# 38 of 43 k tiles of a down projection by seven products: four groups of eight and one of six, in place of a group of four and four of eight

## The chip, the cores and the metric

The kernel runs on one core of a Trainium2 chip. The metric is the device time of one execution in microseconds. Three runs of the kernel before gave 945.45, 945.89 and 946.0; the median is 945.89.

## The reference

One layer of a bidirectional encoder on 256 positions of width 2048, all in float32. Attention and a Fourier mix come first; the change lies in the feed-forward part, which takes some two thirds of the time:

```python
D_FF = ((8 * D_MODEL // 3 + 127) // 128) * 128      # 5504 = 43 x 128

def _conv_ffn(h, w_up, dw_w, dw_b, w_down):
    up = h @ w_up
    gate, val = up[..., :D_FF], up[..., D_FF:]
    gate = lax.conv_general_dilated(
        gate, dw_w, window_strides=(1,), padding=((CONV_WIDTH // 2, CONV_WIDTH // 2),),
        dimension_numbers=('NWC', 'WIO', 'NWC'), feature_group_count=D_FF) + dw_b
    act = jax.nn.gelu(gate, approximate=False) * val
    return act @ w_down
...
    x = x + _conv_ffn(_rmsnorm(x, norm2_g), w_up, dw_w, dw_b, w_down)
    return _rmsnorm(x, normf_g)
```

## The kernel before

**Precision.** Every float32 product is made from two parts of each operand: `hi`, the value rounded to the matmul's input type (a ScalarE copy, L180 or L961), and `lo`, the rest (a VectorE subtraction, L181 or L962). Three matmuls, hi by hi, hi by lo and lo by hi, give the result. Each weight is split so once, after its load, into one of three buffers for hi and one of three for lo.

**Items.** The feed-forward part is a list of items that `ff_items` (L84) writes out by the patterns of L72: `u` is an up unit, `s` a product of a group, `d` a late unit of the down projection. TensorE takes the items in that order.

- An up unit computes the gate or the value columns of one of the 43 k tiles (j): 16 matmuls of 512 columns with hi and 16 of 256 with lo (`still_weights`, L322; its argument `first` says how many of each kind go ahead of the strict alternation). Behind it `up_posts` (L1003) hangs the sums, the convolution, GELU and the product with the value.
- A group of 2n k tiles computes its part of the down projection as a two by two block product by seven products in place of eight, as Strassen's method does, once for each of two column pairs c. A product P1 to P7 or N3 to N5 is 3n matmuls of 512 columns (`by_parts`, L1066). Its stationary operands are sums of activation blocks (`operand`, `operand_sums`). Its weights are sums of four blocks a, b, c, d: these are loaded into a ring of two buffers by SP (`ring_load`, L940); the sum x is begun by VectorE (`first_sums`, L972) and goes on by DMAs that add to it, issued by POOL: d after the split of N5, c after the split of P6 (L965 to L968). P6 reads x after the first of these, N4 after the second. P1 and N5 gather in PSUM over all groups; the others are added up in SBUF after each (`product_out`), and `shared_out` (L1047) joins them at the end.
- The late k tiles go plainly, 24 matmuls a k tile over four column blocks (`moving_weights`, L310); `down_out` adds the result. The late units of c 0 and 1 gather on the banks of the products P2 and N4 of the last group.
- The last three k tiles (40 to 42) come after all items, by four column blocks and two row blocks: `last_product`, nine matmuls each, with final norm and output between them.

**Order.** After item n come, in this order, what was hung `beside` n, the split of item n + 2, and what was hung `behind` n (`ff_step`, L992). Loads of up, late and last weights go through three raw buffers; the load that takes a buffer is issued right behind the split that frees it (L182). The split of the fourth block of last weights (`split_last(3)`) is issued ahead of the third's, which comes with the step of item ("last", 0) after the first `last_product`.

Before, the groups are k tiles 0 to 3, 4 to 11, 12 to 19, 20 to 27 and 28 to 35; 36 to 39 are late.

Of the kernel before, what the change touches and what calls it, by code (L numbers as in the profile page):

```python
# [16 lines left out]
NK = D // P  # L17
# [43 lines left out]
OUT_ORDER += [(c, k) for c in (2, 3) for k in range(4)]  # L61


GROUPS = [(0, 2), (4, 4), (12, 4), (20, 4), (28, 4)]
LATE = list(range(36, 40))
LAST = list(range(40, NF))
PRODUCTS = [
    ["P1", "P7", "N5", "N3", "P6", "P2", "N4"], ["P1", "N5", "P7", "N3", "P6", "P2", "N4"]
]


PATTERNS = ["uuu" + "su" * 13 + "s"] * (len(GROUPS) - 1)  # L72
PATTERNS += ["uuu" + "su" * 6 + "sd" + "su" * 5 + "sdsdd"]


def group_of(j):

    for g, (first, n) in enumerate(GROUPS):
        if j < first + 2 * n:
            return (g, *divmod(j - first, n))  # L80
    return None


def ff_items():  # L84


    def ups(first, end):
        return [(kind, j) for j in range(first, end) for kind in ("gate", "val")]

    firsts = [first for first, _ in GROUPS] + [LATE[0], NF]  # L90
    items = ups(0, firsts[1])
    for g, pattern in enumerate(PATTERNS):
        todo = {
            "u": ups(firsts[g + 1], firsts[g + 2]),
            "s": [("product", g, c, p) for c in range(2) for p in PRODUCTS[c]],
            "d": [("down", c) for c in (0, 2, 1, 3)],
        }
        items += [todo[c].pop(0) for c in pattern]
        assert not (todo["u"] or todo["s"]), (g, todo)
    return items + [("last", c) for c in range(4)]  # L100
# [3 lines left out]
def block_kernel(  # L104
# [6 lines left out]
    w_in: bass.AP,  # L111
    w_out: bass.AP,
    w_up: bass.AP,
    w_down_two: bass.AP,
    w_down: bass.AP,
    w_down_late: bass.AP,
    w_down_last: bass.AP,
    normf_g: bass.AP,
# [16 lines left out]
    def bank(pool, name):  # L135
        return pool.tile([P, 512], F32, tag=pool.name, name=name)


    units = [(w_u_x[i], 2048) for i in range(4)] + [(w_in[i], 2048) for i in range(20)]
# [3 lines left out]
    items, up_index = ff_items(), {}  # L143
    for n, it in enumerate(items):
        if it[0] == "product":
            continue
        up_index[n] = len(units)
        if it[0] in ("gate", "val"):
            units.append((w_up[2 * it[1] + (it[0] == "val")], 2048))
            shifts.append((0, SHIFT))  # L150
            continue
        elif it[0] == "down":
            units.append((w_down_late[it[1]], 2048))
        else:
            units.append((w_down_last[it[1]], 512 * len(LAST)))
        shifts.append((0, 0))
    RAW = 3
    raws, halves = {}, {}
# [100 lines left out]
    ps = bank(dn, "ps_warm")  # L259
# [62 lines left out]
    def still_weights(hi, lo, ps, kk, first=(0, 0)):  # L322

        todo = [list(kk), list(kk)]
        order = [(i, todo[i].pop(0)) for i in range(2) for _ in range(first[i])]
        while todo[0] or todo[1]:
            order += [(i, todo[i].pop(0)) for i in range(2) if todo[i]]  # L330
        for n, (i, k) in enumerate(order):
            x = slice(0, S if i else 2 * S)
            nc.tensor.matmul(  # L333
                ps[:, x], (hi, lo)[i][:, k * P : (k + 1) * P], hk(k)[:, x],
                start=n == 0 and k == 0, stop=n == len(order) - 1 and k == NK - 1,
            )

    def hk(k):
        return hT[k // 4][:, k % 4, :]
# [18 lines left out]
    def at(when, i, f, *a):  # L358
        when.setdefault(i, []).append((f, a))
# [17 lines left out]
    for k in range(NK):  # L377
        c, q = k // 4, k % 4
        if q == 0:
            hi, lo = (t.rearrange("p (k c) -> p k c", k=4) for t in parts_of(c))  # L380
        n = 1 if c < 2 else 2
# [421 lines left out]
    for n, (c, kq) in enumerate(OUT_ORDER):  # L803
# [15 lines left out]
        if kq >= 2:  # L819
            part = "a" if kq == 2 else "f"  # L820
            ps = ps_a[c] if kq < 3 else ps_a[c, "f"]
# [47 lines left out]
    def val_mult(j):  # L869
        va, ge = sums_of.pop(f"v{j}"), gate_out.pop(j)  # L870
        if j >= LATE[0]:
            q = j - LATE[0]
            if q % 2 == 0:
                tag = ("va", "va", "op_P1", "op_N5")[q // 2]
                act["pair"] = fp.tile(
                    [P, 2, 512], F32R, tag=tag, name=f"act_{j}", bufs=3 if tag == "va" else 1
                )
            nc.vector.tensor_tensor(va, va, ge, ALU.mult)
            sums_of[j] = va
            act[j] = act["pair"][:, q % 2, :]  # L880
            return
        g, half, q = group_of(j)
        if q == 0:
            parts[g, half] = fp.tile([P, 4, S], F32, tag="va", name=f"va{g}k{half}", bufs=3)
        nc.vector.tensor_tensor(parts[g, half][:, q, :], va, ge, ALU.mult)
# [18 lines left out]
    def block_of(g, name):  # L904
        k, t = PLACE[name]
        return parts[g, k][:, 0 : GROUPS[g][1], t * P : (t + 1) * P]

    def operand(g, name):

        o = fp.tile([P, 2, 4, P], F32R, tag=f"op_{name}", name=f"op_{name}", bufs=1)  # L910
        o = o[:, :, 0 : GROUPS[g][1], :]
        a = block_of(g, name)
# [15 lines left out]

    ring, ring_tiles = [(g, c, w) for g in range(len(GROUPS)) for c in range(2) for w in "abdc"], {}
    ring_next = [0]  # L930

    def weights_of(g, c, w):
        n = c * 4 + "abcd".index(w)
        return w_down_two[n] if g == 0 else w_down[8 * (g - 1) + n]

    def ring_tile(g, tag, name, bufs):
        t = fp.tile([P, 2048], F32, tag=tag, name=name, bufs=bufs)
# [54 lines left out]
    def ff_step(n):  # L992
        todo, later[:] = list(later), []
        for f in todo:
            next(f, None)
        run(beside, n)
        split_item(n + 2)
        for f in todo:
            for _ in f:
                pass  # L1000
        run(behind, n)

    def up_posts(n, kind, j, ps):  # L1003
# [4 lines left out]
        else:  # L1008
            at(beside, n + 1, scaled_sum, ps, f"v{j}")
            at(beside, n + 2, val_mult, j)  # L1010
            if j + 1 in [first + 2 * n for first, n in GROUPS]:
# [9 lines left out]
                at(behind, n + 7, operand, g, "P6")  # L1021
            if j >= LATE[0]:
                at(behind, n + 2, act_parts, j)
# [109 lines left out]


    pair, joined = [], {}
    for q in range(2):
        kind, j = items[q]
        ps = bank(mm, f"ps_{kind}{j}")
        pair.append((ps, *halves.pop(n_front + q)))
        still_weights(*pair[q][1:], ps, range(12))  # L1140
        if q == 0:
            ff_step(0)
            turn_x(3)
            hT[:] = hT2
# [9 lines left out]
    for n, it in enumerate(items):  # L1154
        if n < 2:
            continue
        if it[0] == "last":
            break
        if n in (2, 3):
            ring_load()  # L1160
        if n == 5:
            pending.append(lambda: first_sums(0, 0))
        if it[0] in ("gate", "val"):
            kind, j = it
            ps = bank(mm, f"ps_{kind}{j}")
            still_weights(*halves.pop(up_index[n]), ps, range(NK))
            ff_step(n)
            up_posts(n, kind, j, ps)
            continue
        if it[0] == "product":  # L1170
            kind, g, c, p = it
            end = g == len(GROUPS) - 1
            if (c, p) in held:
                by_parts(held[c, p], parts[p], *halves.pop(it), GROUPS[g][1], g == 0, end)
            elif end and p in ("P2", "N4"):
                ps = joined[c, p] = bank(mm, f"ps_{p}{g}{c}")
                by_parts(ps, parts[p], *halves.pop(it), GROUPS[g][1], True, False)
            else:
                ps = bank(mm, f"ps_{p}{g}{c}")
                by_parts(ps, parts[p], *halves.pop(it), GROUPS[g][1], True, True)  # L1180
                at(beside, n + 1, product_out, g, c, p, ps)
            if end and p == ("N4", "P6")[c]:
                for q in range(3):
                    at(behind, n + 1 + (1 + c) * q, shared_out, c, q)
        else:
            kind, c = it
            hi, lo = halves.pop(up_index[n])
            if c < 2:
                ps = [joined.pop((c, p)) for p in ("P2", "N4")]
            else:  # L1190
                ps = [bank(mm, f"ps_l{c}{b}") for b in range(2)]
            for b in range(2):
                moving_weights(hi, lo, 512, LATE, act.get, b, ps[b], c >= 2, True)
            at(beside, n + 1, down_out, c, ps)
            if c == 1:
                gfb = fp.tile([P, D], F32, tag="sumw", name="gfb", bufs=1)
                nc.gpsimd.dma_start(gfb, normf_g.partition_broadcast(P))
        ff_step(n)
# [50 lines left out]
def _layout(inp):  # L1249
# [40 lines left out]
    def rows_by(tiles, cols):  # L1290
# [4 lines left out]
    downs = [  # L1295
        rows_by(range(k, k + m), c + n)
        for first, m in GROUPS
        for c in (0, 512)
        for k in (first, first + m)
        for n in (0, 1024)  # L1300
    ]
    late = [rows_by(LATE, 512 * c) for c in range(4)]
    dw = f(inp["dw_w"]).reshape(3, NF, P).transpose(2, 1, 0).reshape(P, 3 * NF)
# [21 lines left out]
        "w_in": win,  # L1325
        "w_out": wout,
        "w_up": wup,
        "w_down_two": np.stack(downs[:8]),
        "w_down": np.stack(downs[8:]),
        "w_down_late": np.stack(late),  # L1330
        "w_down_last": np.stack([rows_by(LAST, 512 * c) for c in range(4)]),
        "normf_g": f(inp["normf_g"]),
# [20 lines left out]
```

## Time and profile before

| what | us |
|---|---|
| median of three runs | 945.89 |
| the profiled execution | 945.47 |
| its span, first to last instruction | 943.7 |
| TensorE busy | 934.7 |
| VectorE busy | 759.8 |
| ScalarE busy | 541.4 |
| POOL busy | 50.6 |

The feed-forward part begins at 255.7 us of the span. In rows of instructions the first number is the start or, in groups, the line; the second is how long it took. In groups, the numbers behind the bar are busy time in us, the mean of one in ns, and the idle time before them with what ended it. In rows of stretches each engine has its busy time and its number of instructions; then come the granted TensorE clock, the busy share of the DMA engines and GB/s. Rows of DMA issues give the size of one and the median time in us from issue to landing. DVE is VectorE, ACT is ScalarE, PE is TensorE and PEld its weight loads.

### The profile page before, as it was taken

What the parts mean: (1) busy time and instruction counts of PE and PEld (TensorE: products, weight loads), DVE (VectorE), ACT (ScalarE), POOL (GpSimd) and SP (SyncE); (2) the same over time, 40 slices, a digit from 0 to 9 for tenths busy, and PEclk for the clock granted to TensorE, in tenths of its full rate; (3) what the DMA queues carried; (4) which work ended last, traced back from release to release, by engine and by line L of the source; (5) the groups of instructions that cost most, each with busy time, mean ns of one, the idle gap of its engine ahead of it and who ended that gap; (6) DMA issues with size and microseconds to landing.
All of it is one profiled execution on the core that took longest, in us unless ns stands there. A gap on an engine that the chain in (4) does not pass through costs nothing.

```text
span 943.7 us, 12802 instructions
## 1 busy us (share of the span) xinstructions
PE 934.7 (99%) x5069; PEld 809.9 (86%) x5069; DVE 759.8 (81%) x948; ACT 541.4 (57%) x659; POOL 50.6 (5%) x67
## 2 busy tenths in 40 slices
PE   9999999999999999999999999999999999999996
PEld 7889998888888888888888888888888888888885
DVE  7658877666677878799887997878989779989886
ACT  7756766454454564566555565555655556655542
POOL 0100000000000000000000000000000000000002
PEclk9999999999999999999999999999999999999999
DMA  9964444446456577877797778777787978779552
GB/s 365 308 224 150 163 147 166 142 171 223 179 220 207 187 238 239 273 249 250 234 276 256 244 228 288 236 262 230 258 246 240 302 234 267 226 244 290 178 178 90
DMA packets 33628, 214.86 MB, mean 228 GB/s; under 512 B 3712, under 2 KB 4224, under 8 KB 10016
## 3 DMA queue, kind: packets, MB, share of 16 engines
q1 hardware_dynamic: 29024, 184.55, 52.9%
q0 software_dynamic: 4544, 29.49, 16.4%
q8 instruction: 40, 0.66, 0.3%
q14 instruction: 20, 0.16, 0.0%
HBM read 211.93 MB, written 2.10 MB: 227 GB/s over the span
## 4 chain that ended last, share of the span: by engine, by line
PE 98%; DVE 1%; DMA 0%; issue 0%; ACT 0%; DVEq 0%; POOLq 0%; POOL 0%; ACTq 0%
PE ps_val L333 25%; PE ps_gate L333 25%; PE ps_q L333 7%; PE ps_P L1071 3%; PE ps_P L1072 3%; PE ps_P L1070 3%; PE ps_N L1071 3%; PE ps_N L1072 3%; PE ps_N L1070 3%; PE ps_a L318 2%; PE ps_a L316 2%; PE ps_k L333 2%; PE ps_a L317 2%; PE ps_s L637 1%; PE ps_o L709 1%; PE ps_ff L316 1%
## 5 line engine op out<-in xcount | busy, mean ns | idle before, releaser
L181 DVE TENSOR_TENSOR lo<-raw,hi 128x2048 fp32r<-128x2048 f32 (+1 forms) x129 | 293.4, 2275 | 40.5 <-ACT hi L180 40.3
L180 ACT ACTIVATE hi<-raw 128x2048 fp32r<-128x2048 f32 (+1 forms) x129 | 245.5, 1903 | 41.5 <-PE ps_a L317 13.5
L333 PE MATMUL ps_val<-hU,hi 128*128 128x512 f32 x688 | 236.6, 390 | 0.0
L333 PE MATMUL ps_gate<-hU,hi 128*128 128x512 f32 x688 | 236.5, 389 | 0.0
L333 PE MATMUL ps_val<-hU,lo 128*128 128x256 f32 x688 | 190.1, 276 | 0.0
L333 PE MATMUL ps_gate<-hU,lo 128*128 128x256 f32 x688 | 190.1, 276 | 0.0
L333 PEld LDWEIGHTS ps_val<-hU,hi 128*128 128x128 f32 x688 | 129.2, 188 | 27.0
L333 PEld LDWEIGHTS ps_gate<-hU,hi 128*128 128x128 f32 x688 | 129.2, 188 | 26.9
L333 PEld LDWEIGHTS ps_val<-hU,lo 128*128 128x128 f32 x688 | 129.2, 188 | 1.3
L333 PEld LDWEIGHTS ps_gate<-hU,lo 128*128 128x128 f32 x688 | 129.2, 188 | 1.3
L845 ACT ACTIVATE ft_g<-ps_gate 128x256 f32<-128x256 f32 x43 | 16.5, 384 | 123.8 <-PE ps_gate L333 123.8
L845 ACT ACTIVATE ft_v<-ps_val 128x256 f32<-128x256 f32 x43 | 16.5, 384 | 91.1 <-PE ps_val L333 91.1
L333 PE MATMUL ps_q<-hT,hi 128*128 128x512 f32 x192 | 65.2, 392 | 0.0
L1071 PE MATMUL ps_P<-hi_P,op_P 128*128 128x512 f32 x144 | 56.2, 390 | 0.0
L1070 PE MATMUL ps_P<-hi_P,op_P 128*128 128x512 f32 x144 | 56.1, 389 | 0.0
L1072 PE MATMUL ps_P<-lo_P,op_P 128*128 128x512 f32 x144 | 56.0, 389 | 0.0
L333 PE MATMUL ps_q<-hT,lo 128*128 128x256 f32 x192 | 51.1, 277 | 0.0
L962 DVE TENSOR_TENSOR lo_N<-sumw,hi_N 128x2048 fp32r<-128x2048 f32 (+1 forms) x20 | 41.5, 2076 | 9.4 <-ACT hi_N L961 9.2
L1071 PE MATMUL ps_N<-hi_N,op_N 128*128 128x512 f32 x108 | 42.1, 390 | 0.0
L1070 PE MATMUL ps_N<-hi_N,op_N 128*128 128x512 f32 x108 | 42.0, 389 | 0.0
L1072 PE MATMUL ps_N<-lo_N,op_N 128*128 128x512 f32 x108 | 42.0, 389 | 0.0
L333 PEld LDWEIGHTS ps_q<-hT,hi 128*128 128x128 f32 x192 | 35.2, 188 | 6.7
(380 smaller groups left out, 1584.2 us busy)
## 6 DMA issues: line engine op xcount, KB each, us to landing
raw<-in_w_up SPq DMA_DIRECT2D x86, 1024.0 KB, 5.7
raw<-in_w_in SPq DMA_DIRECT2D x20, 1024.0 KB, 4.9
raw<-in_w_out SPq DMA_DIRECT2D x16, 1024.0 KB, 4.8
sumw<-in_w_down POOLq DMA_DIRECT2D x16, 1024.0 KB, 8.3
raw<-in_w_down_late SPq DMA_DIRECT2D x4, 1024.0 KB, 6.2
raw<-in_w_down_last SPq DMA_DIRECT2D x4, 768.0 KB, 4.4
ux<-in_w_u_x SPq DMA_DIRECT2D x3, 768.0 KB, 9.4
xs<-in_x SPq DMA_DIRECT2D x4, 512.0 KB, 16.6
```

The lines of the kernel that those rows point to most:

```text
L180: nc.scalar.activation(hi[:, 0:n], raw[:, 0:n], AF.Copy)
L181: nc.vector.tensor_tensor(lo[:, 0:n], raw[:, 0:n], f32(hi[:, 0:n]), ALU.subtract)
L316: nc.tensor.matmul(ps, ah, wh, start=first and q == q0, stop=False)
L317: nc.tensor.matmul(ps, al, wh, start=False, stop=False)
L318: nc.tensor.matmul(ps, ah, wl, start=False, stop=last and q == q0 + len(kk) - 1)
L333: nc.tensor.matmul(ps[:, x], (hi, lo)[i][:, k * P : (k + 1) * P], hk(k)[:, x], start=n == 0 and k == 0, stop=n == len(order) - 1 and k == ...
L637: nc.tensor.matmul(ps[:, b * S : (b + 1) * S], qT[:, qo + b * P : qo + (b + 1) * P], kT[:, ko : ko + S], start=n == 0, stop=n == 2,)
L845: nc.scalar.activation(tmp, ps[:, S : 2 * S], AF.Copy)
L962: nc.vector.tensor_tensor(lo, src, f32(hi), ALU.subtract)
L1070: nc.tensor.matmul(ps, o[:, 0, p, :], hi[:, s], start=first and p == 0, stop=False)
L1071: nc.tensor.matmul(ps, o[:, 1, p, :], hi[:, s], start=False, stop=False)
L1072: nc.tensor.matmul(ps, o[:, 0, p, :], lo[:, s], start=False, stop=last and p == n - 1)
```

## The change

Group 0 gets the size of the others, the last group has six k tiles, and two k tiles stay late. The late units are then 1024 columns of weight each, in place of 2048, and 12 matmuls in place of 24. The patterns are written anew: the first sixteen up units stand ahead of group 0's products, the products of groups 0 to 2 alternate with up units, those of group 3 stand partly two together, those of the last group two or three together, with the late units between them in the order 2, 0, 3, 1. Up units behind the first late unit start with two hi matmuls (`first` is (1, 0)). The number of items is the same. The weights of the last group lie in an array of their own (`w_down_three`, 128 by 1536 a block), which the host writes.

```diff
-GROUPS = [(0, 2), (4, 4), (12, 4), (20, 4), (28, 4)]
-LATE = list(range(36, 40))
+GROUPS = [(0, 4), (8, 4), (16, 4), (24, 4), (32, 3)]
+LATE = list(range(38, 40))
...
-PATTERNS = ["uuu" + "su" * 13 + "s"] * (len(GROUPS) - 1)
-PATTERNS += ["uuu" + "su" * 6 + "sd" + "su" * 5 + "sdsdd"]
+PATTERNS = ["uuu" + "su" * 13 + "s"] * (len(GROUPS) - 2)
+PATTERNS += ["uuu" + "su" + "sussu" * 4 + "s"]
+PATTERNS += ["uuu" + "s" + "su" * 4 + "sdsdu" + "ssusssu" + "sdsd"]
...
-            "d": [("down", c) for c in (0, 2, 1, 3)],
+            "d": [("down", c) for c in (2, 0, 3, 1)],
...
-            units.append((w_down_late[it[1]], 2048))
+            units.append((w_down_late[it[1]], 512 * len(LATE)))
...
-                tag = ("va", "va", "op_P1", "op_N5")[q // 2]
+                tag = ("va", "va", "op_P1")[q // 2]
...
-        return w_down_two[n] if g == 0 else w_down[8 * (g - 1) + n]
+        return w_down[8 * g + n] if GROUPS[g][1] == 4 else w_down_three[n]
...
+    first_late = [it[0] for it in items].index("down")
...
-        if n in (2, 3):
+        if n in (8, 9):
             ring_load()
-        if n == 5:
+        if n == 13:
             pending.append(lambda: first_sums(0, 0))
...
-            still_weights(*halves.pop(up_index[n]), ps, range(NK))
+            first = (1, 0) if n > first_late else (0, 0)
+            still_weights(*halves.pop(up_index[n]), ps, range(NK), first)
```

More of the change, by code (lines that the diff above doesn't have):

```diff
@@ L113, in block_kernel @@
     w_up: bass.AP,
-    w_down_two: bass.AP,
     w_down: bass.AP,
+    w_down_three: bass.AP,
     w_down_late: bass.AP,
@@ L1327, in _layout @@
         "w_up": wup,
-        "w_down_two": np.stack(downs[:8]),
-        "w_down": np.stack(downs[8:]),
+        "w_down": np.stack(downs[:32]),
+        "w_down_three": np.stack(downs[32:]),
         "w_down_late": np.stack(late),
```

## Prediction

> **What bounds the kernel now.** I read the page's engine line first, then busy time by stretch, then the chain of waits.
>
> ```profile
> span 943.7 us, 12802 instructions
> PE 934.7 (99%) x5069; PEld 809.9 (86%) x5069; DVE 759.8 (81%) x948; ACT 541.4 (57%) x659; POOL 50.6 (5%) x67
> ```
> ```profile
> core 0: us, PE busy (x) PEld busy (x) DVE busy (x) ACT busy (x) POOL busy (x), PEclk, DMA share, GB/s
> 656.96:782.08 125.12, 125.12 (x681) 108.78 (x680) 107.08 (x110) 72.15 (x70) 5.15 (x6) 1.00 0.79 252
> 850.08:897.40 47.32, 47.32 (x245) 40.27 (x244) 41.60 (x44) 25.35 (x23) 1.72 (x2) 1.00 0.75 227
> 897.40:919.36 21.96, 21.96 (x99) 18.02 (x97) 19.42 (x23) 10.96 (x9) 0.56 (x1) 1.00 0.55 192
> ```
> TensorE never idles in these stretches (one whole eight-tile group, the last group after its first late unit, the end of the downs). VectorE is next, at 86 to 88%: a bound that is near, not one that is reached.
>
> ```profile
> 425.92 5.44 PE ps_val L333 x32
> 434.08 5.44 PE ps_gate L333 x32
> 858.47 5.60 PE ps_val L333 x32
> 866.85 5.60 PE ps_gate L333 x32
> 891.97 5.60 PE ps_val L333 x32
> ```
> An up unit takes 5.44 us; two starts lie 8.16 apart, so a product of twelve 512-column matmuls takes 2.72, or 0.227 each. From some 856 us on the same units take 5.60.
>
> **Matmuls removed.** Plain down work is 24 such matmuls a k tile (L310), a seven-product group 21. Two tiles move: 6 x 0.227 = **1.36 us less**. That is all that TensorE is spared, and under the 0.2% (1.9 us) that a measurement of this kernel can tell from no change.
>
> **What hides the splits.** Each weight is split by ScalarE (hi), then VectorE (lo), into three buffers. The split of an item can start only when the item three places earlier is done, so it has the time of the two items between.
>
> ```profile
> 496.48 0.39 PE L1070 MATMUL ps_P<-hi_P,op_P 128*128 128x512 f32 x1
> 496.96 1.91 ACT L961 ACTIVATE hi_N<-rawd11d 128x2048 fp32r<-128x2048 f32 x1
> 498.90 2.29 DVE L962 TENSOR_TENSOR lo_N<-rawd11d,hi_N 128x2048 fp32r<-128x2048 f32 x1 [0.92 <-ACT hi_N L961]
> 504.64 0.39 PE L1070 MATMUL ps_N<-hi_N,op_N 128*128 128x512 f32 x1
> ```
> The unit before P7 ends at 496.48; hi starts 0.48 later, lo ends at 501.19: 4.71 us from release. The product starts at 504.64, 3.45 us later. The new patterns shorten this window of 8.16. Two four-tile products make 5.44, which still holds 4.71; two three-tile ones (nine matmuls, 2.04 each) make 4.08, a short late unit and one product 4.76. At the first up unit behind two such products (val 39) lo is late by 4.71 - 4.08, less the 0.23 until it is first read: 0.4 us, and some 0.2 at the next up while VectorE catches up: **+0.6**. The order (1, 0), hi first, allows 0.23 more, but only behind the first down.
>
> **The ledger of the last group.** Durations by kind:
>
> ```profile
> L181 DVE TENSOR_TENSOR lo<-raw,hi 128x2048 fp32r<-128x2048 f32 x17 | 38.8, 2285 | 0.2 <-ACT hi L180 0.2
> L181 DVE TENSOR_TENSOR lo<-raw,hi 128x1536 fp32r<-128x1536 f32 x3 | 5.3, 1754 | 0.6 <-ACT hi L180 0.6
> L1077 DVE TENSOR_TENSOR xs<-ps_l,xs 128x512 f32<-128x512 f32 x4 | 2.6, 683 | 0.0
> L847 DVE TENSOR_TENSOR fa_v<-ps_val,ft_v 128x256 f32<-128x256 f32 x8 | 3.4, 421 | 1.9 <-ACT ft_v L845 1.9
> L859 DVE SCALAR_TENSOR_TENSOR cv<-fa_g,vec,cv 128x255 f32<-128x255 f32 x7 | 3.4, 484 | 0.2
> ```
> ```profile
> L962 DVE TENSOR_TENSOR lo_N<-sumw,hi_N 128x1024 fp32r<-128x1024 f32 x4 | 4.9, 1223 | 0.2
> ```
> I count what stands in VectorE's queue of the changed kernel behind the split of N4 (first column pair), up to and with the lo of the third last block: 3 lo of 2048 columns (6.9), 11 lo and one weight sum of 1536 (21.0), 3 lo of 1024 (3.7), 25 adds of 512 (17.1: 16 of the shared sums, 6 late ones, 3 products), 14 steps of 256 (6.1). Together 54.8 us in 57 instructions. Neighbours overlap by 0.08 (the two lo from 908.04, 2.285 + 1.754, take 3.95 below), so 50.3.
>
> TensorE's time over the same stretch, with no stall: N4 2.04, d 2.72, u 5.44, ss 4.08, u 5.44, sss 6.12, u 5.44, sdsd 9.52, two last products 4.08, plus 0.45 until lo is read: 45.3, plus the lead that N4's lo has, 4.76 less 3.75 (0.48 + 1.49 + 0.03 + 1.75): 46.3 in all. So VectorE is the bound even if it waits for nothing. Before, the same end had late units of 5.44 and products of 2.72 to work behind. And it must wait, at one place above all:
>
> ```profile
> 908.04 3.95 DVE L181 TENSOR_TENSOR lo<-raw,hi 128x2048 fp32r<-128x2048 f32 x2
> 918.85 1.76 DVE L1210 TENSOR_TENSOR lo<-raw,hi 128x1536 fp32r<-128x1536 f32 x1 [1.67 <-ACT hi L1209]
> 921.72 1.75 DVE L181 TENSOR_TENSOR lo<-raw,hi 128x1536 fp32r<-128x1536 f32 x1
> ```
> ```profile
> 917.32 1.49 ACT L1209 ACTIVATE hi<-raw 128x1536 fp32r<-128x1536 f32 x1 [1.94 <-DMA raw<-in_w_down_last]
> 919.36 0.39 PE L1219 MATMUL ps_e<-hi,act 128*128 128x512 f32 x1
> ```
> ```profile
> raw<-in_w_down_last SPq DMA_DIRECT2D x4, 768.0 KB, 4.4
> ```
> Block 3 of the last weights takes the raw buffer that block 0 leaves, so its load starts when the lo of block 0 is done (911.99) and its hi could start at 917.32. The split of block 2 is queued behind block 3's on both engines (918.85, then 921.72 to 923.47), and TensorE reads block 2 at 919.36 + 4.08 + 0.45 = 923.89. It fits by 0.4 us, though block 0 was ready 7.4 us ahead of 919.36.
>
> In the changed kernel, count from the end of the last up unit. TensorE reaches block 0 after 9.52 and needs block 2's lo after 14.05. VectorE ends N4's lo after 3.75, then has one 256 step, a 1024 lo, three 512 adds, one 256 step, two 512 adds and block 0's lo (7.2 less overlaps 0.6): block 0 ready after 10.3, 0.3 late. Load 4.4, hi 1.49, block 3's lo 1.75, two adds 1.3, block 2's lo 1.75: ready after some 20.8. TensorE waits **6.4 us** before the third last product. Meanwhile VectorE idles 4.4 + 1.5 less the 3.0 of work that it has (block 1's lo, two adds): 3.0. For shorter waits on ScalarE, of the kind of the 0.92 above, I add 2.7. 50.3 + 3.0 + 2.7 - 46.3 = **+9.7**, of which 6.7 at the end and 3.0 at the three ups behind short items. Bounds: 4.0 (no wait at all) to 12 (the load takes the 5.3 of 911.99 to 917.32, the other waits 4).
>
> **The weight sums.** The accumulating loads of the x sum go through POOL's queue:
>
> ```profile
> sumw<-in_w_down POOLq DMA_DIRECT2D x16, 1024.0 KB, 8.3
> rawd10b<-in_w_down POOLq DMA_DIRECT2D x1, 1024.0 KB, 9.7
> ```
> In group 3 (pattern sussu) N5 to N4 is 21.76 us of TensorE; before, 32.64. Two rounds of load and split, 2 x (8.3 + 4.23), make 25.1, against 21.76 + 3.45 + 0.45 = 25.7: it holds by 0.6 at 8.3 and misses by 2.2 at 9.7. The splits behind a late N4 are late too. Between 0 and 3.4 I take **+1.0**, nearer to the sixteen loads than to the one. SP's loads follow the splits in the order of use; the four-tile ones of group 0 start later than before, behind plain ups, where VectorE has time.
>
> **The slow units.** 5.60 for 5.44 behind the first late unit: five ups and the products lose 1.4 us. I know no cause. Three ups remain there: a gain of 0 to 1.4, taken at **-0.6**.
>
> **The clock.**
>
> ```profile
> 936.00:940.00 4.00, 0.00 (x0) 0.00 (x0) 3.19 (x7) 0.51 (x1) 0.74 (x2) 1.00 0.45 166
> 940.00:943.70 3.70, 0.00 (x0) 0.00 (x0) 0.06 (x1) 0.00 (x0) 0.00 (x0) 0.54 0.54 205
> ```
> ```profile
> 0.99 3.35 PE L261 MATMUL ps_warm<-ones 128*128 128x128 f32 x14 [0.99 <-POOL ones L253]
> ```
> ```profile
> 4.57 6.01 PE ps_u L395 x24
> ```
> With no matmul from 936 on, the granted clock is full until 940 and about half after: 4 us of idling drop it. An idle 6.4 us does. At the start the warm-up matmuls run from 0.99, and from 4.57 real ones run at 0.25 us each, near full speed: the return takes 3.6 us at most, of which half is lost: 0 to 1.8, taken at **+1.8**.
>
> The Trainium skill ("TensorE: Matmul & The Clock Gate", Part 1: The HAM clock gate) gives one window of about 3.4 us for the fall to half and as much of busy time for the return. By that the drop would come sooner and cost 1.7; the stalls of a us or two before would stay free. The rows agree on the half, and their 4 us is a little over its window.
>
> **Sum.** -1.4 + 0.6 + 9.7 + 1.0 - 0.6 + 1.8 = +11.1 on this execution: span 943.7 to 954.8, time 945.47 to **956.6** (the median of the runs shown is 945.89).
>
> **Rivals.** (a) *VectorE keeps up.* The place is the same end: should the splits stay ahead, 945.47 - 1.4 - 1.4 = 942.7, faster. For it: 12% idle. It decides from 46.3 us of queue; the rows give 50.3. 5%. (b) *The load of block 3 is early enough*, the end costs little and the clock stays: 3.3 left of the 9.7 and no 1.8: 948.4. 12%. (c) *The accumulating loads are slow* (9.7): +2.4 more at group 3, and the ledger at 12: some 961. 10%. (d) *As forecast, but the clock does not fall*: 954.8. 25%. The forecast: 45%. (e) The changed order leaves all as it is, within 0.2%: 3%.
>
> The range 949.5 to 961.0 holds the forecast, (d), most of (c) and part of (b). Faster by over 0.2% is 0.05 (a); within 0.2% 0.03 (e); slower 0.92.
>
> **What would show it.** The chain should leave TensorE at the end: an idle stretch of about 6 us before the third ps_e product, released by VectorE's lo, itself behind a hi that waits for in_w_down_last; a granted clock near half just after; 0.5 to 1.5 us at val 41, gate 42 and val 42; VectorE without a gap there. An end of ps_e without such a gap proves the ledger wrong; late P6 and N4 in group 3 with their hi released by the POOL load would be (c).

## The result: 960.05 us, and the profile after

Four runs of the changed kernel gave 958.32, 960.05, 960.05 and 960.31 us, beside four of the kernel before with a median of 945.67: a ratio of 1.0149, 95% interval 1.0136 to 1.0161. The change made the kernel slower by some 14 us. The time lies 3.5 us above the forecast, near the end of its range. The profiled execution took 960.31 us. Its first lines, as on the page of before:

```profile
span 958.5 us, 12799 instructions
PE 939.9 (98%) x5063; PEld 810.2 (85%) x5063; DVE 763.6 (80%) x946; ACT 543.2 (57%) x657; POOL 50.6 (5%) x67
```

TensorE has six matmuls less, as counted, and is busy 5 us longer. Where it waits, by the view of waits of TensorE from 840 to 937 us (engine and line, what released it, us in all, how often, the longest; ps_e are the last products):

```profile
PE ps_e L1222 <- ACT hi L181: 3.4, 1, 3.4
PE ps_e L1224 <- DVE lo L182: 2.6, 1, 2.6
PE ps_val L334 <- DVE lo L182: 1.5, 3, 0.7
PE ps_gate L334 <- DVE lo L182: 1.2, 1, 1.2
```

Before, this view had nothing in the feed-forward part. For an account to the end I took every item's time from its first matmul to the first of the next item, less 0.2267 us for each 512 columns. What is left over, the item's excess, adds up to 1.47 us in the kernel before and 17.60 after. (A wait costs about 0.3 us more from start to start than the idle time in the view, as 1.04 for 0.73 at N4 of group 3: the view's matmul ends are modelled, and it does not count the slow first matmul.)

| term | forecast | measured |
|---|---|---|
| six matmuls | -1.36 | -1.36 |
| group 3: N4, val 35, P1, gate 36 | +1.0 | +2.2 |
| val 39, gate 40 | +0.6 | +0.7 |
| val 41, gate 42, val 42 | +3.0 | +3.6 |
| the last products: waits, then half clock | +6.7 and +1.8 | +9.0 in all |
| slow units | -0.6 | +0.5 |
| sum | +11.1 | +14.6 (the spans differ by 14.8) |

**The end.** ScalarE and VectorE at the last weights, from the timeline of the changed kernel (start, us, engine, line, operation; in brackets the idle time before it and what ended that):

```profile
920.33 1.49 ACT L181 ACTIVATE hi<-raw 128x1536 fp32r<-128x1536 f32 x1 [0.34 <-PE ps_l L318]
922.40 1.49 ACT L181 ACTIVATE hi<-raw 128x1536 fp32r<-128x1536 f32 x1 [0.58 <-PE ps_N L1072]
930.09 1.48 ACT L1212 ACTIVATE hi<-raw 128x1536 fp32r<-128x1536 f32 x1 [6.20 <-DMA raw<-in_w_down_last]
931.48 1.47 ACT L181 ACTIVATE hi<-raw 128x1536 fp32r<-128x1536 f32 x1
```
```profile
923.92 3.42 DVE L182 TENSOR_TENSOR lo<-raw,hi 128x1536 fp32r<-128x1536 f32 x2
...
931.61 1.76 DVE L1213 TENSOR_TENSOR lo<-raw,hi 128x1536 fp32r<-128x1536 f32 x1 [2.94 <-ACT hi L1212]
933.28 0.68 DVE L1078 TENSOR_TENSOR xs<-ps_P,xs 128x512 f32<-128x512 f32 x1
933.88 0.68 DVE L1078 TENSOR_TENSOR xs<-ps_N,xs 128x512 f32<-128x512 f32 x1
934.48 1.75 DVE L182 TENSOR_TENSOR lo<-raw,hi 128x1536 fp32r<-128x1536 f32 x1
```

This is the queue that the prediction described. Blocks 0 and 1 are split from 923.92 on; block 3's hi (L1212) waits for its transfer until 930.09; its lo, two adds and only then block 2's lo follow, which ends at 936.23. TensorE takes the third last product in two steps: idle until block 2's hi, two matmuls, idle until its lo. The granted clock by stretch:

```profile
core 0: us, PE busy (x) PEld busy (x) DVE busy (x) ACT busy (x) POOL busy (x), PEclk, DMA share, GB/s
929.65:933.00 3.35, 0.00 (x1) 0.00 (x1) 1.39 (x1) 2.86 (x2) 0.00 (x0) 1.00 0.00 0
933.00:936.28 3.28, 0.73 (x2) 0.30 (x2) 3.28 (x5) 0.00 (x0) 0.00 (x0) 0.68 0.00 0
936.28:940.72 4.44, 4.43 (x11) 3.51 (x12) 2.01 (x4) 1.70 (x5) 2.55 (x2) 0.50 0.00 0
940.72:944.50 3.78, 3.78 (x17) 3.15 (x16) 1.73 (x4) 0.47 (x2) 1.40 (x2) 0.96 0.00 0
```

From 936.28 to 940.72 eleven matmuls run where nearly twenty would.

**The ups of the last group.** VectorE from the end of N4's lo (879.23) to the end of its work on block 1:

```profile
core 0: us, PE busy (x) PEld busy (x) DVE busy (x) ACT busy (x) POOL busy (x), PEclk, DMA share, GB/s
879.23:928.67 49.44, 46.88 (x225) 38.09 (x224) 47.61 (x55) 23.46 (x22) 3.13 (x4) 1.00 0.70 205
```

It is busy 96% of that stretch. From 879.23 to 936.23 are 57.0 us; the ledger gave 50.3 + 3.0 + 2.7 = 56.0. Over the whole 57.0 VectorE is busy for 52.2 us (the ledger's 50.3) and idle for 4.8 (its 5.7): two misses that partly cancel.

**Group 3.** The chain of waits around its N4 (start, us, what), then that hi in ScalarE's timeline:

```profile
749.48 8.24 DMA sumw<-in_w_down
...
762.36 8.48 DMA sumw<-in_w_down
...
770.95 1.93 ACT hi_N L962
...
772.90 2.29 DVE lo_N L963
```
```profile
770.95 1.92 ACT L962 ACTIVATE hi_N<-sumw 128x2048 fp32r<-128x2048 f32 x1 [5.54 <-DMA sumw<-in_w_down]
```

From N5's lo (the first load starts 0.3 behind it, at 749.48) to N4's lo (775.19) the x chain takes 26.0 us. TensorE reads that lo 0.45 behind 773.90, which leaves 25.2. N4 itself loses 1.04.

### The profile page after: what moved, and what is told of

It reads as the page before. It is cut to its first block, busy times and chain, and to the rows that moved or that the text cites. A ratio compares the mean times of both kernels' runs of the same rounds, so it can differ in the third digit from the quotient of the medians.

```text
span 958.5 us, 12799 instructions
## 1 busy us (share of the span) xinstructions
PE 939.9 (98%) x5063; PEld 810.2 (85%) x5063; DVE 763.6 (80%) x946; ACT 543.2 (57%) x657; POOL 50.6 (5%) x67
## 4 chain that ended last, share of the span: by engine, by line
PE 89%; DVE 5%; DMA 3%; issue 1%; ACT 1%; DVEq 0%; POOLq 0%; POOL 0%; ACTq 0%
PE ps_gate L334 23%; PE ps_val L334 23%; PE ps_q L334 7%; PE ps_P L1073 3%; PE ps_P L1071 3%; PE ps_P L1072 3%; PE ps_a L319 2%; PE ps_a L317 2%; PE ps_k L334 2%; PE ps_a L318 2%; PE ps_N L1073 2%; PE ps_N L1072 2%; PE ps_N L1071 2%; DVE lo L182 2%; DMA sumw<-in_w_down 2%
## 5 line engine op out<-in xcount | busy, mean ns | idle before, releaser
L182 DVE TENSOR_TENSOR lo<-raw,hi 128x2048 fp32r<-128x2048 f32 (+2 forms) x129 | 289.1, 2242 | 46.4 <-ACT hi L181 46.2
L181 ACT ACTIVATE hi<-raw 128x2048 fp32r<-128x2048 f32 (+2 forms) x129 | 242.0, 1876 | 31.4 <-PE ps_a L318 13.5
L1073 PE MATMUL ps_P<-lo_P,op_P 128*128 128x512 f32 x152 | 59.4, 391 | 0.0
L1072 PE MATMUL ps_P<-hi_P,op_P 128*128 128x512 f32 x152 | 59.3, 390 | 0.0
L1071 PE MATMUL ps_P<-hi_P,op_P 128*128 128x512 f32 x152 | 59.2, 389 | 0.0
L963 DVE TENSOR_TENSOR lo_N<-sumw,hi_N 128x2048 fp32r<-128x2048 f32 (+1 forms) x20 | 43.7, 2183 | 14.3 <-ACT hi_N L962 14.3
L1073 PE MATMUL ps_N<-lo_N,op_N 128*128 128x512 f32 x114 | 44.6, 391 | 0.7 <-DVE lo_N L963 0.7
L1072 PE MATMUL ps_N<-hi_N,op_N 128*128 128x512 f32 x114 | 44.5, 390 | 0.0
L1071 PE MATMUL ps_N<-hi_N,op_N 128*128 128x512 f32 x114 | 44.4, 389 | 0.0
L962 ACT ACTIVATE hi_N<-sumw 128x2048 fp32r<-128x2048 f32 (+1 forms) x20 | 36.5, 1826 | 9.1 <-DMA sumw<-in_w_down 7.8
```

What stands on the lines that cost most here:

```text
L181: nc.scalar.activation(hi[:, 0:n], raw[:, 0:n], AF.Copy)
L182: nc.vector.tensor_tensor(lo[:, 0:n], raw[:, 0:n], f32(hi[:, 0:n]), ALU.subtract)
L962: nc.scalar.activation(hi, src, AF.Copy)
L963: nc.vector.tensor_tensor(lo, src, f32(hi), ALU.subtract)
L1071: nc.tensor.matmul(ps, o[:, 0, p, :], hi[:, s], start=first and p == 0, stop=False)
L1072: nc.tensor.matmul(ps, o[:, 1, p, :], hi[:, s], start=False, stop=False)
```

## The experiments

All but e12 are edits of the changed kernel. Each was timed beside the kernel before; medians and ratios:

| run | us | ratio to before, 95% |
|---|---|---|
| the changed kernel | 960.05 | 1.0149 (1.0136 to 1.0161) |
| e1 block 2 first | 954.14 | 1.0087 (1.007 to 1.0104) |
| e3 group 3's order | 957.62 | 1.0125 (1.011 to 1.014) |
| e4 sums late | 960.79 | 1.0166 (1.015 to 1.0181) |
| e5 clock kept | 958.11 | 1.0132 (1.0117 to 1.0147) |
| e6 order of items | 953.3 | 1.0079 (1.0065 to 1.0093) |
| e7 order of items, block 2 first | 947.21 | 1.0022 (1.0011 to 1.0032) |
| e8 group of six first | 945.86 | 1.0002 (0.9993 to 1.0011) |
| e9 group of six first, sums late | 949.58 | 1.0038 (1.0025 to 1.0051) |
| e10 block 3 loaded early | 956.34 | 1.0119 (1.0102 to 1.0136) |
| e11 hi and lo in turn | 959.28 | 1.0147 (1.0132 to 1.0162) |
| e12 before, block 2 first | 945.64 | 1.0001 (0.9992 to 1.0011) |
| e13 group of six first, all else as changed | 954.39 | 1.0094 (1.0079 to 1.0109) |

### e1: block 2's split ahead of block 3's

```diff
         if (c, b) == (0, 0):
             ff_step(items.index(("last", 0)))
+            split_last(3)
         last_post(c, b, ps, o, n)
...
-    split_last(3)
     for c in range(4):
         last_product(c, 0)
```

> The changed kernel, but the split of block 2 of the last weights is queued ahead of the split of block 3 on ScalarE and VectorE. Queue theory (block 2 stands behind block 3, whose load starts only when block 0's lo is done): the idle time of 3.4 + 2.6 us before the third ps_e product shrinks to between 1 and 2 us, too short for the granted clock to fall, so about 4.8 us of waiting and 2.2 us at half clock go: 953.3 us. Rival, VectorE's amount of work alone sets the end and the order does not matter: only the 2.9 us in which VectorE has nothing to do (928.7 to 931.6) can be won, some 957.4 us, with TensorE waiting at block 3 in place of block 2. No change at all would be 960.3.

954.14, 5.9 us less than the changed kernel. One wait is left at the end (waits of TensorE):

```profile
PE ps_e L1224 <- DVE lo L182: 1.5, 1, 1.5
```

The last products' excess falls from 9.23 to 2.36 us; group 3's grew by half a microsecond in this execution (1.57 at N4 for 1.04). The order of two splits, with nothing taken away, is worth two fifths of the loss, 5.9 of 14.4 us: the rival's 957.4 is out.

### e10: block 3 loaded early, same order of splits

```diff
         if p in ("P1", "P7", "N3", "P2"):
             ring_load()
+            if p == "P2" and (g, c) == (len(GROUPS) - 1, 1):
+                i = len(units) - 1
+                raws[i] = fp.tile([P, 2048], F32, tag="rawd", name=f"raw{i}", bufs=2)
+                nc.sync.dma_start(raws[i][:, 0 : units[i][1]], units[i][0])
...
-        hi = fp.tile([P, 2048], F32R, tag="rawd", name=f"hi{i + c}")
+        hi = wp.tile([P, 2048], F32R, tag="raw", name=f"hi{i + c}", bufs=RAW)
```

> The changed kernel, but block 3 of the last weights is loaded into a ring buffer as soon as the last product weights are split, and its hi goes into the raw buffer that block 0 leaves; the order of the splits is as in the changed kernel. Queue theory: hi of block 3 no longer waits for a transfer of 4.4 us but still for block 0's lo, and block 2 still stands behind it on VectorE: the wait for block 2 falls from 6.0 to about 3.3 us, too short for the clock to fall: about 955 us, less than the order alone gave (954.1). Rival, the transfers are held up by one another: an earlier load delays block 1 or 2 and the wait stays near 6 us: 959 to 960.

956.34: the wait is 3.2 us, as the queue theory has it, but the time is 1.3 above its 955. The clock fell after all in the profiled execution (955.5 us):

```profile
core 0: us, PE busy (x) PEld busy (x) DVE busy (x) ACT busy (x) POOL busy (x), PEclk, DMA share, GB/s
929.03:932.19 3.16, 0.00 (x1) 0.00 (x1) 3.16 (x5) 0.00 (x0) 0.00 (x0) 1.00 0.00 0
932.19:936.20 4.01, 4.01 (x11) 3.17 (x12) 2.01 (x4) 1.69 (x5) 2.29 (x2) 0.57 0.00 0
```

An idle 3.16 us, which I had taken for too short, was followed by half clock; that costs 1.5 us here (4.01 less eleven matmuls of 0.2267). Two other executions took 957.17 and 957.55 us; why, is open.

### e5: the clock kept up

28 matmuls that nobody reads stand ahead of the third ps_e product:

```diff
         ps = bank(dn, f"ps_e{c}{b}{o}")[:, 0:n]
+        for _ in range(28 if (c, b) == (2, 0) else 0):
+            nc.tensor.matmul(
+                ps, act[LAST[0]][:, 0:P], halves[i + 1][0][:, 0:512], start=True, stop=True
+            )
```

> The changed kernel with 28 more matmuls ahead of the third ps_e product, into its own bank, which the product then overwrites: 6.35 us of work in place of idle time. It computes nothing that is kept. Theory (the idle time lets the granted clock fall to half, and that costs about 2.2 us after the wait): the clock stays full from 930 to 945 us and the time falls by 2.0 to 2.3 us, to 958.1. Rival, the half clock is only a mark in the record, or the matmuls after the wait are slow for another cause: no gain, 960.3; matmuls that come too late to be free would add to it.

958.11, and the stretches of the end at full clock:

```profile
929.90:936.50 6.60, 6.60 (x31) 5.37 (x30) 5.22 (x5) 2.69 (x3) 0.00 (x0) 1.00 0.00 0
936.50:940.50 4.00, 4.00 (x19) 3.31 (x18) 1.97 (x4) 2.17 (x6) 2.87 (x3) 1.00 0.02 4
```

So the fall of the clock costs about 1.9 us of the total (2.0 to 2.3 expected), and is not only a mark in the record.

### e4: half of the shared sums' adds behind the last splits

`shared_out` is regrouped: four adds that read PSUM in step 0, four of SBUF alone in step 1.

```diff
-                for q in range(3):
-                    at(behind, n + 1 + (1 + c) * q, shared_out, c, q)
+                at(behind, n + 1, shared_out, c, 0)
...
     for c in range(4):
         last_product(c, 0)
+        if c < 2:
+            shared_out(c, 1)
```

> The changed kernel, but of the eight adds of each column pair's shared sums only the four that read PSUM stay where they are; the other four run behind the split of the last block 2. Ledger theory (VectorE's queue is the bound between val 41 and the end): about 2.5 us leave the queue ahead of gate 42, whose stall falls from 1.65 to about 0.5, and 2.5 more ahead of block 0, so that the wait at the end falls by 1.4 too: about 957.5 us. Rival, the loads and not VectorE's amount of work set the end: gate 42 comes sooner, but the wait at the end stays or grows by as much, 959 to 960.3 us. If the adds, now behind the last splits, hold up the last sums: some tenths more.

960.79: a miss. Gate 42 did as expected (1.65 to 0.43 us of excess), and the last product ends 2.3 us sooner (948.4 for 950.7; 15.1 us in the account for 17.6). But the wait for block 2 stayed, and the end behind the last product grew from 7.8 to 10.8 us. The wait first, by the timelines of ScalarE and VectorE and the chain of waits:

```profile
927.61 1.48 ACT L1208 ACTIVATE hi<-raw 128x1536 fp32r<-128x1536 f32 x1 [6.24 <-DMA raw<-in_w_down_last]
```
```profile
929.12 1.76 DVE L1209 TENSOR_TENSOR lo<-raw,hi 128x1536 fp32r<-128x1536 f32 x1 [5.96 <-ACT hi L1208]
```
```profile
921.38 6.21 DMA raw<-in_w_down_last
```

VectorE was done with blocks 0 and 1 early and had nothing to do for 5.96 us: block 3's load, issued 3.2 us behind block 2's (5.0 in the changed kernel), took 6.21 us in place of the 4.37 of the changed kernel (925.70 to 930.07). At this place the transfer sets the end, not VectorE's amount of work. The longer end is taken up in the last section.

### e3: group 3 in another order

```diff
-PATTERNS += ["uuu" + "su" + "sussu" * 4 + "s"]
+PATTERNS += ["uuu" + "sussususususussusssusus"]
```

> The changed kernel with another order of the same items beside group 3: no product of the first column pair between N5 and N4 stands next to another one, the four doubled places are N4 P1, P1 N5 and so on in the second column pair, where the x chain has time. Theory (the two accumulating loads and splits between N5 and N4 need some 26 us, the changed kernel gives 25): N4 and the three units behind it lose their 2.1 us of stalls, 958.2 us; if the slow units from 787 to 856 us (5.60 in place of 5.44) are an after-effect of those stalls, 1.3 us more, 956.9. Rival, VectorE is simply behind in this group: the stalls move to other units and the time stays at 960.3.

Products now stand side by side at P7 N5, then at P1 N5 and P7 N3 P6 of the second column pair (not at N4 P1, which the expectation names: an up stands between them). 957.62, 2.4 us less: the stalls at N4, val 35, P1 and gate 36 are gone. Slow units appear all the same, from 806 us on, behind a wait of about 0.1.

### e6 and e7: another order of items, without and with block 2 first

```diff
-PATTERNS += ["uuu" + "su" + "sussu" * 4 + "s"]
-PATTERNS += ["uuu" + "s" + "su" * 4 + "sdsdu" + "ssusssu" + "sdsd"]
+PATTERNS += ["uuususususussusususssususs"]
+PATTERNS += ["uuusussussdsusussdussdsususd"]
```

In e7 the last string ends in "dusssduussd", the downs go 3, 0, 2, 1, and e1's edit is in.

> The changed kernel with nothing but another order of the same items: in group 3 no doubled products between N5 and N4 of the first column pair, in the last group the ups are spread so that two of them stand among the last ten items, and the downs go 2, 0, 3, 1. Theory (short items without an up beside them leave the splits no cover; the same amount of work fits where every run of short ones has an up behind it): the stalls of group 3 go, of the 3.6 us at val 41, gate 42 and val 42 about 1 is left, the wait for block 2 falls from 6.0 to about 4 and stays too short for the clock: some 951 us. Rival, VectorE's amount of work from N4 on is the bound whatever the order: what is won ahead of the downs comes back at the end, 957 us or more.

> The changed kernel with both: the order of items of the run before with the downs 3, 0, 2, 1, and the split of block 2 ahead of that of block 3. Theory: what is left is some 0.5 us each at gate 40, val 41 and block 2, the slow units' 1.5 and half a us at the very end: 946 to 947 us. If the two causes are not independent (VectorE behind in the last group, and the load of block 3), the sum of the single gains is not reached: 948 or more.

e6: 953.3. The ups from val 39 on together lose 1.5 us in place of 4.3, so most of VectorE's work does fit when the runs of short items are broken up. Group 3 is not free of stalls: N4 of the second column pair has an excess of 0.6 us and gate 38 behind it one of 0.5, behind accumulating loads of 9.98 and 8.77 us. The median is 2 us above the expected 951, but the four executions are of two kinds: 954.61 and 954.56 us at a mean granted clock of 0.994 and 0.995, and 952.04 and 951.8 at 0.996 and 0.997. The profiled one is the slowest; in it the clock fell too, though no single wait was longer than 2.6 us (0.9, 1.1 and 2.6 us by the view of waits, with matmuls between):

```profile
922.53:930.57 8.04, 3.54 (x14) 2.29 (x14) 5.50 (x7) 2.86 (x2) 0.00 (x0) 0.88 0.08 34
930.57:935.42 4.85, 4.85 (x11) 3.79 (x12) 2.00 (x4) 2.12 (x6) 2.55 (x2) 0.50 0.00 0
```

e7: 947.21, just above the expected 946 to 947. The two edits add up: 5.9 (e1) and 6.75 (e6) make 12.7, and e7 is 12.84 below the changed kernel, though its order of items is not quite that of e6.

### e13, e8, e9: the group of six tiles first

```diff
-GROUPS = [(0, 4), (8, 4), (16, 4), (24, 4), (32, 3)]
+GROUPS = [(0, 3), (6, 4), (14, 4), (22, 4), (30, 4)]
...
-PATTERNS = ["uuu" + "su" * 13 + "s"] * (len(GROUPS) - 2)
-PATTERNS += ["uuu" + "su" + "sussu" * 4 + "s"]
+PATTERNS = ["uuu" + "su" * 13 + "s"] * (len(GROUPS) - 1)
```

e13 is this alone, with the ring's first loads and first sum moved to earlier items. e8 has e1's edit too and "uuusussuussdsusussdusssdsusd" in the last group; e9 has besides four adds of the second pair's shared sums behind the last splits, and an order of its own.

> The changed kernel with the group of six tiles moved to the front (groups of eight at the end), all other things as in the changed kernel: the same order of ups, products and downs in the last group, block 3 ahead of block 2, two late tiles. Theory (the order of the last group and block 3's load make most of the cost, not the size of the last group's products): group 3's stalls go, since all groups ahead are plain pairs, but val 41 and gate 42 still wait 1.0 and 1.4 us and block 2 some 6 us with the clock falling: about 956 us. Rival, the short products of 2.04 us at the end are what VectorE cannot follow: with products of 2.72 the stalls and the wait go: 946 to 948 us.

> The same 38 tiles by seven products, but the group of six tiles comes first, as the group of four did before the change, and four groups of eight follow; two late tiles, an order of the last group with an up near each run of short items, block 2 ahead of block 3. Theory: with the products of 2.72 us at the end and plain pairs of product and up in all groups ahead, nothing waits but the first last product for the act of tile 42 (about 1.3 us); the 1.36 us of removed matmuls pay that: 945.5 to 946 us, as before the change. Rival, the short late units and not the group's place make the cost: stalls of 3 us or more in the last group as in the changed kernel, 949 us.

> As the run before, with the second half of the shared sums' adds of the second column pair behind the last split, those of the first pair three items behind their N4, and an order of the last group that goes with it. Theory: no stall is left in the feed-forward part, the late adds cost about 0.9 us at the very end; with the slow units (1.5 us) 945 us, without them 943.7: between 0 and 2 us faster than before the change. If the adds at the end cost as much as they did in the run with all sums late (3.0 us): 947.

e13: 954.39. Group 3 has no stall, but val 41 and gate 42 still lose 1.1 and 1.2 us, and the end 8.75, with the same two waits:

```profile
PE ps_e L1221 <- ACT hi L180: 3.2, 1, 3.2
PE ps_e L1223 <- DVE lo L181: 2.5, 1, 2.5
```

The short products of the last group are not the cause of the end: with products of 2.72 us and the same order it is nearly as bad (8.75 for 9.23). At the ups they do count: val 39 and val 42, which lose 0.65 and 0.99 us in the changed kernel, lose nothing here. e8: 945.86, no difference from before that the runs can tell. The feed-forward part has no wait left but one:

```profile
span 944.2 us, 12800 instructions
PE 933.6 (99%) x5063; PEld 807.7 (86%) x5063; DVE 763.8 (81%) x946; ACT 543.7 (58%) x657; POOL 51.0 (5%) x67
```
```profile
919.04 0.39 PE L1221 MATMUL ps_e<-hi,act 128*128 128x512 f32 x1
920.20 0.50 PE L1222 MATMUL ps_e<-hi,act 128*128 128x512 f32 x1 [0.78 <-DVE act L890]
```

TensorE is busy 1.1 us less than before the change. What the six matmuls spare goes into this wait for the act of tile 42 and into a longer end behind the last product (8.6 us, 944.2 less 935.6; before 7.75, 943.7 less 935.95), both work of VectorE. e9, the attempt to take adds out of VectorE's way, missed: 949.58 for 945 to 947. Its only waits in the feed-forward part are of 0.7 and 0.2 us; most of the loss is in the end behind the last product, 10.8 us (8.6 in e8).

### e12 and e11: two controls

e12 is e1's edit in the kernel before. e11 lets all units begin with hi and lo in turn:

```diff
-            first = (1, 0) if n > first_late else (0, 0)
+            first = (0, 0)
```

> The kernel before, with the split of block 2 of the last weights queued ahead of that of block 3, as in the run of the changed kernel that won six microseconds. Theory: before the change block 0 was split early enough, so the order cost nothing there: 945.4 to 945.9 us, the same. Rival, the order is worth something by itself: 944.5 or less. If block 3 then comes late: up to 947.

> The changed kernel, but the units behind the first down begin with hi, lo, hi, lo as they did before the change, not with two of hi. Theory: lo is read 0.23 us sooner by val 41, gate 42 and val 42, where it is late, so val 41 and val 42 each wait some 0.2 us more and the end keeps its waits: 0.3 to 0.7 us more, 960.4 to 960.8. Rival, VectorE's queue alone sets the end, so a wait that comes sooner is only the same wait: no change, 960.05.

e12: 945.64, the same as before: the order of the two splits costs nothing as long as block 0 is split 7 us early. e11: val 41 and val 42 lose 0.3 us more each and gate 42 0.2 less; the time (959.28) is not above the changed kernel's. The edit is worth less than these runs can tell.

## Why the prediction was right, point by point

**Matmuls removed.** Right: 5063 for 5069, and 1.1 us less busy time where nothing waits (e8).

**The ledger of the last group.** Right in size at the three ups: 3.6 us for 3.0, released by VectorE's lo at each. e6 makes them small by another order; e4, with work taken away, does so at gate 42 alone, and val 41 and val 42 keep their 1.0. What VectorE loses by waiting for block 3 (3.0 forecast) is 2.94 in the timeline. The ledger's "VectorE is the bound even if it waits for nothing", a floor of 4.0 us, holds for this order of items as far as it was tried, and not for the amount of work. e1, with all the work left in, still loses 3.5 us at the three ups and 2.4 at the end, above that floor; but e7, the same work with other orders of items and splits, loses 2.5 from gate 40 to the end. And e4 took adds out of the queue and the wait for block 2 stayed, since block 3's transfer then took longer. By the sum of their gains there are two causes, nearly independent: runs of short items without an up among them (e6), and block 2 queued behind a split that waits for a transfer (e1, e10).

**The clock.** The size is right: 1.8 forecast, 1.9 by e5. The reading "4 us of idling drop it" failed as a threshold, and so did the thought that stalls of a us or two stay free. By stretches cut finer, the clock fell at 932.7 us in e10, 0.5 behind an idle 3.16; at 934.2 in the changed kernel, 1.2 behind an idle 3.35, with two matmuls and 0.45 of the next wait between; and at 928.7 in e6, after waits of 0.9 and 1.1 us and 0.7 of a third. It then stayed at half for 3.4 us in e10 and for 6.8 in the other two. The Trainium skill ("TensorE: Matmul & The Clock Gate", Part 1: The HAM clock gate) says that the window of some 3.4 us runs freely and does not reset when a kernel starts. The two kinds of executions of e6 fit that: the same waits cost the clock more or less, depending on where the window lies. How much of a window must be idle, no run here shows. The rows of the changed kernel:

```profile
933.00:934.18 1.18, 0.73 (x2) 0.30 (x2) 1.18 (x3) 0.00 (x0) 0.00 (x0) 1.00 0.00 0
934.18:936.28 2.10, 0.00 (x0) 0.00 (x0) 2.10 (x3) 0.00 (x0) 0.00 (x0) 0.50 0.00 0
```

**The weight sums.** The step that failed is "it holds by 0.6 at 8.3". The loads took 8.24 and 8.48, so the loads' time was right and rival (c), slow loads, did not come (it came in e6, where a load of 9.98 us stood in the chain). What I left out is the way between: POOL starts a load 0.3 us behind the lo that it waits for, ScalarE begins 0.1 behind the landing, twice each, and N5 had a lead of 2.96 (752.14 less 749.18) in place of 3.45. So 26.0 stood against 25.2, not 25.1 against 25.7. Late as N4 was, the three units behind it lost another 1.2 us. (In e1, e5, e10 and e11 N4 alone lost 1.4 to 1.6, in place of 1.04.) e3 shows that the place of the doubled products is the cause.

**The slow units.** The step "three ups remain there: a gain of 0 to 1.4" failed: the slow units cost 0.5 us more than before. In the changed kernel six ups of 5.60 us stand ahead of the first late unit. The chain of waits has the same two units in the changed kernel and in e4, at the same place:

```profile
798.14 5.60 PE ps_val L334 x32
806.52 5.60 PE ps_gate L334 x32
```
```profile
798.02 5.44 PE ps_val L334 x32
806.18 5.44 PE ps_gate L334 x32
```

Both stand behind the stalls of group 3, and one is slow, the other not. So no late unit is needed for it. In the kernel before, which has no wait in the feed-forward part, it begins at the first late unit, so no wait is needed either. Why, stays open, and it was not tried by itself.

**The rivals.** (a) and (b) need an end without the wait for block 2; they are what e7 and e8 had to build. (d), no fall of the clock, is e5: 958.1 in place of 954.8, since group 3 (2.6 us for 1.0) and the ups behind it (4.5 for 3.6) cost more than its sum had.

## What to carry to other kernels

Ask what one wait holds up behind it in an in-order queue: two splits exchanged were worth 6 us here, and nothing in the kernel before, where the same queue had 7 us of lead. Work that is hidden behind long items has to be counted per stretch when items get shorter; an order with a long item near every run of short ones cost nothing and gave back most of the rest. A chain across engines and queues needs its hand-overs in the sum (0.1 to 0.3 us each here), where a margin is 0.6.

## What the runs showed of the hardware

**Adds beside POOL.** In e9 VectorE's adds of two SBUF operands took 1.20 and 1.66 us while POOL multiplied, and 0.69 and 0.68 right after; the timelines of VectorE and POOL:

```profile
926.74 1.20 DVE L1058 TENSOR_TENSOR xs<-xs,z_P 128x512 f32<-128x512 f32 x1
927.97 1.66 DVE L1059 TENSOR_TENSOR z_P<-z_P,z_P 128x512 f32<-128x512 f32 x1
929.67 0.69 DVE L1060 TENSOR_TENSOR xs<-xs,z_P 128x512 f32<-128x512 f32 x1
930.28 0.68 DVE L1061 TENSOR_TENSOR xs<-xs,z_P 128x512 f32<-128x512 f32 x1
```
```profile
926.10 1.29 POOL L1098 TENSOR_TENSOR xs<-xs,gfb 128x512 f32<-128x512 f32 x1 [13.73 <-ACT junkc L1086]
927.72 1.37 POOL L1098 TENSOR_TENSOR xs<-xs,gfb 128x512 f32<-128x512 f32 x1 [0.33 <-ACT junkc L1086]
```

The Trainium skill ("SBUF — State Buffer", SBUF: two separate sides) says that POOL and a VectorE instruction with two SBUF inputs share a port pair that one of them holds for a whole instruction. That agrees with these rows. The adds that were moved behind the last splits, in e4 as in e9, met POOL's multiplications with the final norm's weights, and the end behind the last product took 10.8 us in both (7.8 in the changed kernel, 8.6 in e8). How much of that is the port and how much the added work was not tried by itself.

**A state of TensorE 3% slower at full granted clock.** An up unit takes 5.60 in place of 5.44 us for tens of microseconds, 0.2333 for 0.2267 per 512 columns, with the granted clock at 1.00. Kernels that differ only near the end have it at different places. In the changed kernel it begins at the stalls of group 3 and ends in gate 40, which has no wait; in the kernel before it begins at the first late unit.
